# Latent attention interleaved with the mLSTM heads, and mLSTM products padded to 128 rows

## The chip, the cores and the metric

The kernel runs on one core of a Trainium2 chip. The metric is the time of one execution on the device, in microseconds (us). The core has a matrix engine (TensorE, PE in the profile; PEld is its weight load), a vector engine (VectorE, DVE), a scalar engine (ScalarE, ACT), a general engine (GpSimd, POOL) and SyncE (SP), which issues most of the transfers here. Each engine runs its own instructions in order and waits for the others through semaphores.

## What is computed

Two blocks of two layers each, on 512 tokens of 1024 features. The change lies in the first block's mixer, which runs once in each of its two layers. The mixer projects its input into three branches, concatenates their outputs and multiplies by `w_out`; a mixture of 16 experts follows. Cut to the two branches that matter here:

```python
def _mla(...):                       # latent attention, 8 heads, 64 + 32 features for q and k
    q = rmsnorm(c_q) @ w_uq;  kv = rmsnorm(c_kv) @ w_ukv
    s = q_nope @ k_nope + q_rope @ k_rope      # k_rope is shared by all heads
    y_a = softmax(s * scale) @ v

def _mlstm_scan(q, k, v, ig, lf):    # 4 heads of 64 features, run forward and backward
    qk  = (q @ k.T) * w_intra        # inside a chunk
    num = qk @ v + w_inter * (q @ C) # C: state carried from chunk to chunk
    h   = num / max(abs(den), exp(-m))
```

The third branch (a state-space scan, `ssd_` in the code) ends before the stage of interest.

## The kernel before

The 512 tokens are four tiles of 128 (`NT = 4`), and products of the projections are made of three fp16 products each (`mm3`, lines 147 to 151), since every fp32 operand is split into a high and a low fp16 half (`split`, lines 143 and 144; `wsplit` for weights, lines 133 and 134). A layer's `mixer1` runs: projection of latents and gates, the `ssd_` branch, `mlstm_proj` (its last product is `gvo`), then four times `mlstm_head`, then `mla`, then `proj_out` (`gO`). The code is written in this order, but a scheduler fixes the order of instructions on each engine when the program is built, so neighbouring parts overlap. Tiles come from pools with a fixed number of buffers: a tile's next use waits until all readers of the old one are done. PSUM tiles have tags: `acc` and `acm` (sums of projections, `sM`), `s` (`diag`, `sT`) and `o` (`lo`, `o`, `mxT`, `mixT`), two buffers each.

`mlstm_head` (one head h): heads 0 and 1 lie in partitions 0 to 63 and 64 to 127 of the same tiles, as do 2 and 3; `r` is the head's half. `vw` (L1016) and `mlU` (L1022) give the chunk states, which ACT (L1030) and DVE (L1032) chain into `mst`, in the half `r` only. `decays` loads `dk` by a transfer on SP (L856), POOL adds two masks (L859), ACT takes exponentials (L862). `blocks` makes `diag` (L870), four products of 64 rows, which DVE multiplies into `dk` (L1039). For each direction, `lo` sums `dk` times `v` (L1044, 128 rows) and, for three of four tiles, `qs` times `mst` (L1046, 64 rows). DVE then makes the denominator (L1050 to L1053) and writes `mo` (L1056, or L1059 and L1060). An fp32 product stands as two instructions in the trace. `mlstm_norm` normalises a pair of heads, `mix_part` transposes it (`mixT`) into `mT`, the operand of `gO`.

`mla` splits its weights, makes values (`gV`), and goes through four groups of two heads. `project(g)` makes `gQ`, `gK` and the maxima over keys (`sM`, `mx` on DVE, `mxT`). Then, for each head, `softmax_T` makes scores `sT`, `pe` and `pt` (L748, L751, L752), and `pv` makes `o`. The shared rope part of the keys is copied into `Kt` (`mlak`) by eight POOL copies (L672). Group g + 1 is projected ahead of the softmax of group g. The argument `also` of `mla` runs the normalisation of the second mLSTM pair after the first projection.

Of the kernel before, what the change touches and what calls it, by code (L numbers as in the profile page):

```python
# [11 lines left out]
F32 = mybir.dt.float32  # L12
F16 = mybir.dt.float16
BF16 = mybir.dt.bfloat16
I32 = mybir.dt.int32
AF = mybir.ActivationFunctionType
# [5 lines left out]
P = 128  # L22
T = 512
NT = 4
# [21 lines left out]
class Kern:  # L46
# [374 lines left out]
    def mixer1(self, l, cur):  # L421
        p1 = self.p1
        pr = self.params1(l)
        xh, xl = cur["xT"]
        self.mT = self.xT_tiles(p1, "mT")
        u = 1.0 / (AS * WS_IN)

        def load(key, i, n):
            return [self.wload(self.ap[key][l, i, h] if i is not None else self.ap[key][l, h],
                               4 * n, WS_IN) + (4,) for h in range(2)]  # L430

        r = lambda name: self.pool(name, side="right")
        cA = load("wA", None, 472)
        with self.pool("la") as la:
            with r("qa") as self.qa:
                with r("gp") as self.gp:
                    pa = self.qa.tile([P, NT, 472], F32, name="pa")
                    ss = p1.tile([P, 2, NT], F32, name="ss")
                    junk = self.gp.tile([P, 256], F32, tag="g4", name="junk")
                    for t in range(NT):  # L440
                        ps = self.tm_gemm(xh, xl, cA, 472, t, "gA", "acc")
                        self.nc.scalar.activation(pa[:, t, :], ps[:, :472], AF.Copy, scale=u)
                        self.nc.scalar.activation(junk[:, :256], pa[:, t, 0:256], AF.Square,
                                                  accum_out=ss[:, 0, t:t + 1])
                        self.nc.scalar.activation(junk[:, :128], pa[:, t, 256:384], AF.Square,
                                                  accum_out=ss[:, 1, t:t + 1])
                    with ExitStack() as es:
                        for i in cur.get("after", ()):
                            es.enter_context(self.tc.issue_after(i))
                        cD = load("wB", 2, 512)  # L450
                        cC = load("wB", 1, 512)
                    self.gates1(l, pr, pa)
                lat = self.mla_latents(la, pr, pa, ss)
            with r("qm") as qm, r("m1") as m1:
                with r("s1") as self.q1, r("s2") as s2:
                    sd = self.ssd_tiles()
                    for b in (2, 4, 0, 3, 5, 1):
                        self.ssd_conv(b, pr, xh, xl, cC, cD, sd, u)
                    self.ssd_gate(xh, xl, cC, sd, u)
                    c0, c1 = (self.ssd_core(s2, m1, g, pr, sd, u) for g in range(2))  # L460
                    for c in (c0, c1, c0, c1, c0, c1, c0, c1):
                        next(c, None)
                cE = load("wB", 3, 512)
                cB = load("wB", 0, 512)
                ml = self.mlstm_proj(qm, pr, xh, xl, cE, cB, u)
                mo = [self.p2.tile([P, NT, P], F32, tag="mo", name="mo", bufs=2) for i in range(2)]
                og = ml[-1]
                for h in range(4):
                    self.mlstm_head(m1, h, mo[h // 2], *ml)
                    if h > 1:  # L470
                        (self.mlstm_norm(0, mo[0], og) if h == 2 else self.mix_part(p1, 4, mo[0]))
                with r("ml") as p:
                    self.ptp, self.npt = p, (6, 2)
                    self.mla(p, l, lat, lambda: (self.mlstm_norm(1, mo[1], og), self.mix_part(p1, 5, mo[1])))

    def gates1(self, l, pr, pa):

# [173 lines left out]
                self.split(krh[0][64:128], krh[1][64:128], ps[64:128], AS)  # L651
        return cq, ckv, krh

    def mla(self, p1, l, lat, also):
        nc, p2 = self.nc, self.p2
        cq, ckv, krh = lat
        wq = [self.wload(self.ap["w_uq"][l], 2048, WS_UQ) + (2,)]
        wkv = [self.wload(self.ap["w_ukv"][l], 1024, WS_UKV) + (1,)]
        v = self.values(p1, "mlav", 8, 64, 0, 8)
        for t in range(NT):  # L660
            ps = self.acc("gV")
# [3 lines left out]
        scale = 96.0 ** -0.5  # L665
        HG = 2
        Q, K = {}, {}

        Kt = [[p1.tile([P, T], F16, name="mlak%d%d" % (h, i)) for i in range(2)] for h in range(4)]
        for h in range(4):  # L670
            for i in range(2):
                nc.gpsimd.tensor_copy(Kt[h][i][64:128], krh[i][64:128])  # L672

        def project(g):

# [19 lines left out]
            return mrow  # L695

        mrow = project(0)
        also()
        for g in range(8 // HG):
            nrow = project(g + 1) if (g + 1) * HG < 8 else None  # L700
            for i, h in enumerate(range(g * HG, (g + 1) * HG)):
                pt = self.softmax_T(
                    lambda s, ps, st: [
                        self.mm3(ps, K[h][0][:, s * P:(s + 1) * P], K[h][1][:, s * P:(s + 1) * P],
                                 Q[h][0], Q[h][1], True, False),
                        nc.tensor.matmul(ps, self.sel[:, i, :], mrow, start=False, stop=True)],
                    scale, [0] * NT, v[0] is None)
                o = self.pso("o")
                for t in range(NT):
                    self.pv(o[:, t * 66:t * 66 + 65], [(pt[s], t, self.value(v, s, h)) for s in range(NT)])  # L710
                if h % 2 == 0:
                    mx_ = p2.tile([P, NT, P], F32, tag="mo", name="mo", bufs=2)
                self.norm_out(o, 66, 64, mx_[:, :, 64 * (h % 2):64 * (h % 2) + 64])
                if h % 2:
                    self.mix_part(p1, h // 2, mx_)
            mrow = nrow
# [282 lines left out]
    def mlstm_head(self, p1, h, mo, q, k, kt, v, og):  # L999
        nc, p2 = self.nc, self.p2  # L1000
        i, r = h // 2, slice(64 * (h % 2), 64 * (h % 2) + 64)
        if h % 2 == 0:

            self.qs = p1.tile([P, 2, T], F32, tag="mqs", name="mqs", bufs=2)
            for j in range(2):
                nc.sync.dma_start(self.qs[64 * j:64 * j + 64].rearrange("p d t -> p (d t)"),
                                  self.d_wi[h + j:h + j + 1].rearrange("h d t -> h (d t)").partition_broadcast(64))
            for d_ in range(2):
                ts = slice(P * (1 - d_), P * (4 - d_))
                nc.vector.tensor_tensor(self.qs[:, d_, ts], self.qs[:, d_, ts], q[i][:, ts], op=ALU.mult)  # L1010
            self.mst = p1.tile([P, NT, 2, 66], F32, tag="mst", name="mst", bufs=2)

        vw = p1.tile([P, NT, 2, 66], F32, tag="vw", name="vw", bufs=1)
        for d_ in range(2):
# [3 lines left out]
        ps, c, U = self.psx("mlU"), 0, {}  # L1018
# [8 lines left out]
        for d_ in range(2):  # L1027
            ts = (1, 2, 3) if d_ == 0 else (2, 1, 0)
            step = 1 if d_ == 0 else -1
            nc.scalar.activation(self.mst[r, ts[0], d_], U[ts[0] - step, d_], AF.Copy)  # L1030
            for t in ts[1:]:
                nc.vector.scalar_tensor_tensor(self.mst[r, t, d_], self.mst[r, t - step, d_],  # L1032
                                               self.dec[r, 2 * d_, h, t - step:t - step + 1], U[t - step, d_],
                                               op0=ALU.mult, op1=ALU.add)
        dk = self.decays(p1, self.d_nc[0], h, 0)
        ps = self.blocks(k[i][r], q[i][r])
        for d_ in range(2):
            e = dk[:, d_].rearrange("p c i -> p (c i)")
            nc.vector.tensor_tensor(e, ps, e, op=ALU.mult)  # L1039
            o = self.pso("lo")  # L1040
            for t in range(NT):
                inter = self.DST[t][0] <= d_ < self.DST[t][1]
                c = slice(t * 66, t * 66 + 65)
                nc.tensor.matmul(o[:, c], dk[:, d_, t], v[:, t, h, :65], start=True, stop=not inter)  # L1044
                if inter:
                    nc.tensor.matmul(o[:, c], self.qs[r, d_, t * P:(t + 1) * P], self.mst[r, t, d_, :65],  # L1046
                                     start=False, stop=True)
            o3 = o[:, :NT * 66].rearrange("p (t d) -> p t d", t=NT)
            den = self.sm.tile([P, NT, 1], F32, tag="den", name="den")
# [943 lines left out]
```

## Time and profile before

| | us |
|---|---|
| median of 3 runs (lowest to highest) | 2487.95 (2486.26 to 2492.34) |
| the profiled execution, its span | 2485.69, 2483.9 |
| PE busy | 2268.1 (91%) |
| DVE busy | 1698.7 (68%) |
| ACT busy | 1163.8 (47%) |
| POOL busy | 241.0 (10%) |

The span is one execution's from first to last instruction; the shares are means over stages with different limits. Matmuls are pipelined and their ends are modelled, so the distance between two starts says more of PE than a duration does. The stage of the change, from the last `gvo` to the end of the latent attention, lies at 162.6 to 290 us in layer 0 and at 704.1 to 835.5 us in layer 1.

### The profile page before, as it was taken

The numbers are of one execution on the slowest core, as the hardware profiler recorded it, in microseconds if no ns is written. First come the engines' busy times: TensorE is split into PE (matmuls) and PEld (weight loads), VectorE is DVE, ScalarE is ACT, GpSimd is POOL, SyncE is SP. The second block draws the span as 40 slices with busy tenths as digits, with TensorE's granted clock in tenths as the row PEclk, the third lists the DMA queues.
The fourth block names the chain that finished last, engine by engine and source line by source line (L and its number), as shares of the span: only waits on it lengthen the run. The fifth ranks groups of instructions, "written<-read, shape, count | busy, mean of one in ns | idle before, by whom it ended". The sixth has DMA issues, their size and how long they took to land.

```text
span 2483.9 us, 34670 instructions
## 1 busy us (share of the span) xinstructions
PE 2268.1 (91%) x13330; PEld 1239.8 (50%) x13334; DVE 1698.7 (68%) x3668; ACT 1163.8 (47%) x1981; POOL 241.0 (10%) x295
## 2 busy tenths in 40 slices
PE   7898979888898979879898899999998989999999
PEld 4554545544564545534455654444444556544444
DVE  7968887778949877768999664442469996644421
ACT  5534737755625637834554543331245546333321
POOL 1220022221200013221000100000000000000000
PEclk9988989999979979989999999999999999999999
DMA  5320458973210549953210152222331101522222
GB/s 181 122 74 1 166 188 261 338 246 103 96 66 18 213 152 313 341 182 105 80 53 35 49 209 106 102 102 77 119 132 52 52 34 60 187 102 102 102 77 77
DMA packets 57695, 315.25 MB, mean 127 GB/s; under 512 B 9652, under 2 KB 9908, under 8 KB 29104
## 3 DMA queue, kind: packets, MB, share of 16 engines
q1 hardware_dynamic: 40448, 263.67, 29.7%
q0 software_dynamic: 12464, 32.48, 5.2%
q10 hardware_dynamic: 4608, 16.78, 1.8%
q8 instruction: 108, 1.77, 0.3%
q14 instruction: 67, 0.55, 0.1%
HBM read 286.59 MB, written 30.90 MB: 128 GB/s over the span
## 4 chain that ended last, share of the span: by engine, by line
PE 39%; DVE 10%; ACT 4%; issue 2%; DMA 1%; DVEq 0%; ACTq 0%
PE fd L149 3%; PE fd L151 3%; PE fd L150 3%; PE fu L151 3%; PE fg L151 3%; PE fg L150 3%; PE fu L150 3%; PE fg L149 3%; PE fu L149 3%; PE o L787 2%; DVE wl L134 1%; PE gqk L149 1%; DVE mx L1784 1%; PE gqk L151 1%; PE gqk L150 1%
## 5 line engine op out<-in xcount | busy, mean ns | idle before, releaser
L134 DVE SCALAR_TENSOR_TENSOR wl<-wst,wh 128x1024 f16<-128x1024 f32 (+1 forms) x428 | 517.2, 1236 | 211.4 <-ACT wh L133 210.1
L133 ACT ACTIVATE wh<-wst 128x1024 f16<-128x1024 f32 (+1 forms) x428 | 430.0, 1048 | 283.4 <-PE fd L151 107.0
L150 PEld LDWEIGHTS <-wh 128*128 128x128 f16 x968 | 96.1, 99 | 105.4 <-issue 8.3
L151 PEld LDWEIGHTS <-wl 128*128 128x128 f16 x968 | 96.0, 99 | 102.9 <-issue 4.7
L149 PEld LDWEIGHTS <-wh 128*128 128x128 f16 x968 | 96.0, 99 | 101.7 <-issue 4.6
L149 PE MATMUL fd<-wh,fhh 128*128 128x512 f16 x352 | 133.4, 379 | 0.0
L150 PE MATMUL fd<-wl,fhh 128*128 128x512 f16 x352 | 133.4, 379 | 0.0
L151 PE MATMUL fd<-wh,fhl 128*128 128x512 f16 x352 | 133.4, 379 | 0.0
L149 PE MATMUL gqk<-wh,xTh 128*128 128x512 f16 x320 | 123.0, 384 | 6.5 <-ACT rsq L1668 6.2
L150 PE MATMUL gqk<-wl,xTh 128*128 128x512 f16 x320 | 123.0, 384 | 0.0
L151 PE MATMUL gqk<-wh,xTl 128*128 128x512 f16 x320 | 122.8, 384 | 0.0
L149 PE MATMUL fg<-xTh,wh 128*128 128x512 f16 x320 | 121.3, 379 | 0.0
L150 PE MATMUL fg<-xTl,wh 128*128 128x512 f16 x320 | 121.3, 379 | 0.0
L151 PE MATMUL fg<-xTh,wl 128*128 128x512 f16 x320 | 121.3, 379 | 0.0
L149 PE MATMUL fu<-xTh,wh 128*128 128x512 f16 x320 | 121.3, 379 | 0.0
L150 PE MATMUL fu<-xTl,wh 128*128 128x512 f16 x320 | 121.3, 379 | 0.0
L151 PE MATMUL fu<-xTh,wl 128*128 128x512 f16 x320 | 121.3, 379 | 0.0
L150 PEld LDWEIGHTS <-xTh 128*128 128x128 f16 x768 | 74.8, 99 | 70.4 <-issue 12.2
L149 PEld LDWEIGHTS <-xTh 128*128 128x128 f16 x768 | 74.7, 99 | 68.2 <-ACT xTh L143 5.8
L151 PEld LDWEIGHTS <-xTl 128*128 128x128 f16 x768 | 74.4, 99 | 64.6 <-issue 3.5
L149 PE MATMUL gO<-wh,mTh 128*128 128x512 f16 x256 | 98.4, 385 | 2.8 <-ACT mTh L143 2.8
L1843 DVE SCALAR_TENSOR_TENSOR fth<-fth,fg 128x512 f32<-128x512 f32 x40 | 27.5, 687 | 107.5 <-ACT fth L1842 107.5
(612 smaller groups left out, 5516.9 us busy)
## 6 DMA issues: line engine op xcount, KB each, us to landing
wst<-in_w_gu SPq DMA_DIRECT2D x108, 1024.0 KB, 6.2
wst<-in_w_dn SPq DMA_DIRECT2D x52, 1024.0 KB, 9.7
wst<-in_w SPq DMA_DIRECT2D x28, 1024.0 KB, 4.8
wst<-in_wB SPq DMA_DIRECT2D x16, 1024.0 KB, 4.9
wst<-in_w_out SPq DMA_DIRECT2D x16, 1024.0 KB, 4.8
dk<-d_nc SPq DMA_DIRECT2D x16, 512.0 KB, 3.7
rows<-xrow SPq DMA_DIRECT2D x8, 512.0 KB, 2.6
res<-xa SPq DMA_DIRECT2D x8, 512.0 KB, 2.7
```

What stands on the lines that cost most here:

```text
L133: nc.scalar.activation(wh[:, a:b], st[:, a:b], AF.Copy, scale=scale)
L134: (eng or nc.vector).scalar_tensor_tensor(wl[:, a:b], st[:, a:b], scale, wh[:, a:b], op0=ALU.mult, op1=ALU.subtract)
L149: mm(out, ah, bh, start=start, stop=False)
L150: mm(out, ah, bl, start=False, stop=False)
L151: mm(out, al, bh, start=False, stop=stop)
L787: mm(out, p[:, bs], v, start=first, stop=last)
L1784: nc.vector.tensor_reduce(mr[:, t, h:h + 1], ps[:, :n], axis=AX.X, op=ALU.max)
L1843: nc.vector.scalar_tensor_tensor(th, th, 1.0, pg, op0=ALU.add, op1=ALU.mult)
```

## The change

`mla` becomes a generator that stops ahead of each of its four groups. `mixer1` starts it first (weights, values, the first projection), and then takes mLSTM heads and attention groups in turn. The eight key copies move to the front of `mla`. In `mlstm_head`, the operands `q` and `mst` get a zeroed other half, made by POOL, so that `diag` and the second product of `lo` run over 128 rows; `mst` becomes one tile per head. `pt` has five buffers instead of six, and the attention's `mo` moves to a pool with one buffer of its own. The `ml` pool, which holds `Kt`, `pt` and the new `mqz` (one buffer), opens ahead of the heads.

```diff
@@ mixer1
-                for h in range(4):
-                    self.mlstm_head(m1, h, mo[h // 2], *ml)
-                    if h > 1:
-                        (self.mlstm_norm(0, mo[0], og) if h == 2 else self.mix_part(p1, 4, mo[0]))
                 with r("ml") as p:
-                    self.ptp, self.npt = p, (6, 2)
-                    self.mla(p, l, lat, lambda: (self.mlstm_norm(1, mo[1], og), self.mix_part(p1, 5, mo[1])))
+                    self.ptp, self.npt = p, (5, 2)
+                    mla = self.mla(p, l, lat)
+                    next(mla)
+                    for h in range(4):
+                        self.mlstm_head(m1, h, mo[h // 2], *ml)
+                        if h > 1:
+                            (self.mlstm_norm(0, mo[0], og) if h == 2 else self.mix_part(p1, 4, mo[0]))
+                        if h == 3:
+                            self.mlstm_norm(1, mo[1], og)
+                        next(mla, None)
+                    self.mix_part(p1, 5, mo[1])
+                    for _ in mla:
+                        pass
@@ mla
+        Kt = [[p1.tile([P, T], F16, name="mlak%d%d" % (h, i)) for i in range(2)] for h in range(4)]
+        for h in range(4):
+            for i in range(2):
+                nc.gpsimd.tensor_copy(Kt[h][i][64:128], krh[i][64:128])
...
         mrow = project(0)
-        also()
         for g in range(8 // HG):
+            yield
             nrow = project(g + 1) if (g + 1) * HG < 8 else None
...
-                    mx_ = p2.tile([P, NT, P], F32, tag="mo", name="mo", bufs=2)
+                    mx_ = p1.tile([P, NT, P], F32, tag="mo", name="mo")
@@ mlstm_head
-            self.mst = p1.tile([P, NT, 2, 66], F32, tag="mst", name="mst", bufs=2)
+        z = slice(64 * (1 - h % 2), 64 * (1 - h % 2) + 64)
+        qz = self.ptp.tile([P, T], F32, tag="mqz", name="mqz")
+        nc.gpsimd.memset(qz[z], 0.0)
+        nc.gpsimd.tensor_copy(qz[r], q[i][r])
+        mst = p1.tile([P, NT, 2, 66], F32, tag="mst", name="mst", bufs=2)
+        nc.gpsimd.memset(mst[z], 0.0)
...
-        ps = self.blocks(k[i][r], q[i][r])
+        ps = self.blocks(k[i], qz)
...
-                    nc.tensor.matmul(o[:, c], self.qs[r, d_, t * P:(t + 1) * P], self.mst[r, t, d_, :65],
+                    nc.tensor.matmul(o[:, c], self.qs[:, d_, t * P:(t + 1) * P], mst[:, t, d_, :65],
                                      start=False, stop=True)
```

What the scheduler makes of it shows in the order of instructions. On PE, right behind `gvo`, the heads stood together before (`mv` is v, `mqs` is `qs`):

```order
L1044 MATMUL lo<-mv,dk 128x65 x2
L870 MATMUL diag<-ml_1312,ml_1366 128x128 x2
L1046 MATMUL lo<-mst,mqs 128x65
L1044 MATMUL lo<-mv,dk 128x65 x2
L1022 MATMUL mlU<-vw,mkt 128x66
L870 MATMUL diag<-ml_1339,ml_1399 128x128
L1046 MATMUL lo<-mst,mqs 128x65
L1044 MATMUL lo<-mv,dk 128x65
```

In the changed kernel, all of `gV` and the first projection come first, and the first head's `lo` (now L1058 and L1060) stands between the second projection and the first scores:

```order
L736 MATMUL mxT<-idf,mx 128x128 x4
L1058 MATMUL lo<-mv,dk 128x65 x2
L1060 MATMUL lo<-mst,mqs 128x65
L1058 MATMUL lo<-mv,dk 128x65
L1060 MATMUL lo<-mst,mqs 128x65
L1058 MATMUL lo<-mv,dk 128x65
L1060 MATMUL lo<-mst,mqs 128x65
L151 LDWEIGHTS wl
L151 MATMUL gQ<-cq_586,wl 128x512
L1058 MATMUL lo<-mv,dk 128x65
L714 LDWEIGHTS sel
L714 MATMUL sT<-mrow,sel 128x512
```

Each head's products thus moved from one block behind `gvo` into a gap of the attention's. On DVE, the first head's denominator stood among other instructions of the heads:

```order
L1050 TENSOR_SCALAR den<-lo 128x4
L1032 SCALAR_TENSOR_TENSOR mst<-mst,dec,mlU 64x66
L1051 TENSOR_TENSOR den<-den,lo 128x4
L1032 SCALAR_TENSOR_TENSOR mst<-mst,dec,mlU 64x66
L1052 TENSOR_TENSOR den<-den,flo 128x4
L1039 TENSOR_TENSOR dk<-diag,dk 128x512
L1053 RECIPROCAL den<-den 128x4
L1050 TENSOR_SCALAR den<-lo 128x4
L1056 TENSOR_TENSOR mo<-lo,den 128x4x64
```

Now (L1064 to L1070) it stands among the attention's products and a weight split:

```order
L1064 TENSOR_SCALAR den<-lo 128x4
L1046 SCALAR_TENSOR_TENSOR mst<-mst,dec,mlU 64x66
L1065 TENSOR_TENSOR den<-den,lo 128x4
L690 TENSOR_TENSOR qtmp<-gQ,tab 128x512
L1066 TENSOR_TENSOR den<-den,flo 128x4
L134 SCALAR_TENSOR_TENSOR wl<-wst,wh 128x1024
L1067 RECIPROCAL den<-den 128x4
L1064 TENSOR_SCALAR den<-lo 128x4
L1070 TENSOR_TENSOR mo<-lo,den 128x4x64
```

The attention's `qtmp` moved up between the chain's steps. On POOL, the additions of the last two heads (`dk`) and the memsets of `mx` followed the key copies directly:

```order
L672 COPY mlak_1883<-krh_591 64x512
L859 TENSOR_TENSOR dk<-dk,m_lt 128x512
L859 TENSOR_TENSOR dk<-dk,m_gt 128x512
L859 TENSOR_TENSOR dk<-dk,m_lt 128x512
L859 TENSOR_TENSOR dk<-dk,m_gt 128x512
L720 MEMSET mx 128x512 x3
```

Now the padding stands among them, in the same queue:

```order
L1022 MEMSET mqz 64x512
L1023 COPY mqz<-ml_1312 64x512
L728 MEMSET mx 128x512
L1025 MEMSET mst 64x528
L867 TENSOR_TENSOR dk<-dk,m_lt 128x512
L867 TENSOR_TENSOR dk<-dk,m_gt 128x512
L728 MEMSET mx 128x512
L1022 MEMSET mqz 64x512
L1023 COPY mqz<-ml_1339 64x512
L1025 MEMSET mst 64x528
```

The third head's additions now stand behind the second head's `mqz` and the memset of `mst`, and the memsets of `mx` alternate with them.

## Rows read from the trace of the kernel before

**Rows 1.** Windows, layer 0: stretch, length, busy PE PEld DVE ACT POOL, clock, DMA.
```profile
162.60:205.00 42.40, 41.08 (x194) 32.35 (x193) 24.10 (x82) 12.54 (x47) 5.28 (x4) 0.71 0.14 50
205.00:213.00 8.00, 5.70 (x19) 2.21 (x18) 7.03 (x21) 3.01 (x5) 0.00 (x0) 0.71 0.00 0
213.00:290.00 77.00, 69.26 (x653) 36.09 (x651) 69.31 (x130) 52.87 (x105) 2.71 (x5) 0.99 0.16 56
162.60:290.00 127.40, 116.03 (x862) 70.66 (x860) 100.43 (x233) 68.42 (x157) 7.99 (x9) 0.88 0.15 50
```

**Rows 2.** The same windows of layer 1.
```profile
704.10:750.00 45.90, 44.58 (x191) 34.89 (x189) 22.59 (x81) 12.54 (x47) 5.15 (x4) 0.63 0.12 46
...
757.00:835.50 78.50, 70.27 (x656) 36.69 (x655) 70.22 (x132) 53.29 (x106) 2.69 (x5) 0.98 0.16 55
704.10:835.50 131.40, 119.55 (x859) 73.41 (x858) 98.37 (x231) 68.24 (x157) 7.83 (x9) 0.84 0.14 49
```

**Rows 3.** Windows in the heads of layer 0; the clock is the number before DMA's.
```profile
170.00:175.00 5.00, 5.00 (x34) 3.98 (x32) 3.47 (x14) 0.22 (x1) 0.00 (x0) 1.00 0.25 93
180.00:185.00 5.00, 5.00 (x20) 4.00 (x20) 1.77 (x8) 1.52 (x6) 0.00 (x0) 0.50 0.27 97
```

**Rows 4.** Timeline of PE, heads of layer 0: start us, us, instruction, count.
```profile
170.67 0.44 PE L1044 MATMUL lo<-mv,dk 128*128 128x65 f32 x2
171.04 0.43 PE L1046 MATMUL lo<-mst,mqs 64*128 64x65 f32 x2
...
180.21 0.69 PE L1044 MATMUL lo<-mv,dk 128*128 128x65 f32 x2
180.83 0.69 PE L1046 MATMUL lo<-mst,mqs 64*128 64x65 f32 x2
```

**Rows 5.** Timeline of PE: fp32 products of 128 rows and of 64.
```profile
118.75 1.00 PE L932 MATMUL so<-xs,spe 128*128 128x64 f32 x8
119.58 0.38 PE L151 MATMUL gE<-xTh,wl 128*128 128x512 f16 x1
...
99.60 1.28 PE L870 MATMUL diag<-bc 128*128 128x128 f32 x10
...
163.06 1.16 PE L870 MATMUL diag<-ml,ml 64*128 64x128 f32 x10
```

**Rows 6.** Lines 720 and 672: duration in ns, min/median/max.
```profile
L720 POOL MEMSET mx<- x16: 524/524/543, 5.3 to 2057.7; 128x512 f32 x16
...
L672 POOL COPY mlak<-krh x16: 604/623/1624, 132.8 to 677.6; 64x512 f16<-64x512 f16 x16
```

**Rows 7.** Timeline of POOL in the heads of layer 0.
```profile
176.13 1.27 POOL L859 TENSOR_TENSOR dk<-dk,m_lt 128x512 f32<-128x512 f32 x1 [37.58 <-DMA dk<-d_nc]
...
186.12 1.27 POOL L859 TENSOR_TENSOR dk<-dk,m_lt 128x512 f32<-128x512 f32 x1 [7.37 <-ACT mst L1030]
```

**Rows 8.** Timeline of DVE in the heads of layer 0.
```profile
173.59 0.36 DVE L1016 TENSOR_TENSOR vw<-mv,wec 128x198 f32<-128x198 f32 x1
...
175.17 0.42 DVE L1060 TENSOR_TENSOR mo<-mo,ltmp 128x256 f32<-128x256 f32 x1
...
176.38 1.24 DVE L1016 TENSOR_TENSOR vw<-mv,wec 128x198 f32<-128x198 f32 x1
...
186.22 1.45 DVE L1060 TENSOR_TENSOR mo<-mo,ltmp 128x256 f32<-128x256 f32 x1
```

**Rows 9.** Timeline of ACT in the attention.
```profile
228.60 0.63 ACT L751 ACTIVATE pt<-pe 128x512 f16<-128x512 f32 x1
```

**Rows 10.** Waits of SP's queue, 260 to 560 us: us in total, times, longest.
```profile
SPq L122 <- DVE eth L1418: 21.1, 2, 18.5
```

**Rows 11.** Timeline of DVE, first head of layer 0.
```profile
169.16 0.16 DVE L1050 TENSOR_SCALAR den<-lo 128x4 f32<-128x4 f32 x1 [1.48 <-PE lo L1046]
...
172.68 0.41 DVE L1056 TENSOR_TENSOR mo<-lo,den 128x256 f32<-128x256 f32 x1
```

More of the change, by code (lines that the diff above doesn't have):

```diff
@@ L652, in mla_latents, with mla @@
         return cq, ckv, krh
-    def mla(self, p1, l, lat, also):
+    def mla(self, p1, l, lat):
         nc, p2 = self.nc, self.p2
         cq, ckv, krh = lat
+        Kt = [[p1.tile([P, T], F16, name="mlak%d%d" % (h, i)) for i in range(2)] for h in range(4)]
+        for h in range(4):
+            for i in range(2):
+                nc.gpsimd.tensor_copy(Kt[h][i][64:128], krh[i][64:128])
         wq = [self.wload(self.ap["w_uq"][l], 2048, WS_UQ) + (2,)]
@@ L667, in mla @@
         Q, K = {}, {}
[L669 to L672, printed above, removed]
         def project(g):
@@ L1029, in mlstm_head @@
             step = 1 if d_ == 0 else -1
-            nc.scalar.activation(self.mst[r, ts[0], d_], U[ts[0] - step, d_], AF.Copy)
+            nc.scalar.activation(mst[r, ts[0], d_], U[ts[0] - step, d_], AF.Copy)
             for t in ts[1:]:
-                nc.vector.scalar_tensor_tensor(self.mst[r, t, d_], self.mst[r, t - step, d_],
+                nc.vector.scalar_tensor_tensor(mst[r, t, d_], mst[r, t - step, d_],
                                                self.dec[r, 2 * d_, h, t - step:t - step + 1], U[t - step, d_],
```

## The prediction

> **What bounds the kernel now.** I read the windows of each layer's mixer first, from the last `gvo` product to the end of the latent attention: 162.6 to 290 us in layer 0 and 704.1 to 835.5 us in layer 1 [rows 1, 2]. The reader should see two halves. In the first, the four mLSTM heads, PE is busy nearly all the time (41.08 of 42.40 us, 44.58 of 45.90) while DVE works only 24.10 and 22.59 us. In the last, the attention's groups, DVE and PE are each busy 90% (69.31 and 69.26 of 77.00 us), and DVE, whose busy time is not stretched by modelled ends, sets the pace. Over the whole stage DVE works 100.43 of 127.40 us and 98.37 of 131.40 us: 27.0 + 33.0 = 60.0 us in which the second half's bound stands idle, most of it in the first half.
>
> Then the PE timeline of the heads, for why PE is full there. PE's clock is not the same throughout: 1.00 in 170 to 175 us, then 0.50, the lower of the two levels, in 180 to 185 us [rows 3]; ahead of the fall PE had been busy all the time, but with small fp32 products that alternate between 128 rows (L1044) and 64 rows (L1046). A pair of instructions of either kind starts 0.37 us after the pair before it at full clock, and 0.62 us at half clock [rows 4]. Eight instructions of nearly the same size that are all 128 rows (`so`, 64 columns) take 119.58 - 118.75 = 0.83 us, so 0.21 us a pair [rows 5]. Alternating costs 0.16 us a pair at full clock and, against 0.42, 0.20 us at half clock.
>
> The Trainium skill, page "TensorEngine Tiling (Array Packing)", section "Tiling Modes", says that changing the tiling mode drains TensorE. The trace agrees [rows 4, 5]: by the rule the padded products go at 0.21 us a pair, which is what the rows gave without it.
>
> **The change part by part.**
>
> *Padding.* Per layer, 4 heads x 2 directions x (4 + 3) products x 2 instructions = 112 instructions, 56 pairs, of which about 48 stand at a switch: 48 x 0.16 = 7.7 us of PE at full clock. Ten `diag` products of 64 rows took 1.16 us and ten of 128 rows 1.28 us [rows 5], 0.012 us each, so the 32 padded ones per layer cost at most 0.4 us: nothing. PE's work in the heads, told in full-clock time, is 41.08 x 0.71 = 29.2 us [rows 1]; less 7.7 it is 21.5, below DVE's 24.10. For the whole stage: 116.03 x 0.88 - 7.7 = 94.4 us and 119.55 x 0.84 - 7.7 = 92.7 us, both below DVE's 100.43 and 98.37 [rows 1, 2]. So DVE becomes the bound of the stage, if the order lets it.
>
> *Interleaving.* It adds no DVE, ACT or PE work. It puts the attention's DVE work (products' maxima, splits) into the heads' stretch, and the heads' short chains between them; the order of DVE and PE shows it. What share can DVE then reach? The nearest row is the stretch where this already happens with other work, 0.90 (69.31 of 77.00; 70.22 of 78.50 in layer 1). At 0.90 the stages last 111.6 and 109.3 us: -15.8 and -22.1, together -37.9 us. PE then needs 94.4 of 111.6 us, 0.85, less than the 0.90 it shows now in that stretch. The bounds are a share of 1.00 (-60.0 us) and today's 0.79 and 0.75 (nothing).
>
> *POOL.* New per layer: four `mqz` memsets and four copies, and four `mst` memsets, two of which stand ahead of the stage. A 128x512 fp32 memset took 0.524 us and a 64x512 fp16 copy 0.623 [rows 6]; the fp32 copy I bound above by POOL's 128x512 fp32 addition, 1.27 us [rows 7]. Six memsets and four copies: 5.6 to 8.2 us of POOL. POOL itself is idle there, so the cover is its own idle time. But DVE pays: while POOL ran its additions at 176.13 and 186.12 us, a `vw` product of 0.36 us took 1.24 and a `mo` addition of 0.42 took 1.45 [rows 7, 8]: 1.9 us lost to 5.28 us of POOL work. At that rate 2.0 to 3.0 us per layer; I take 3. The eight `mlak` copies stand at the same place in POOL's queue as before, ahead of the stage; that edit is worth nothing.
>
> *Buffers.* Five `pt` tiles instead of six, and one `mo` tile for the attention instead of two: no row shows the wait. Below: nothing. Above: each of 8 heads waits once for a conversion of 0.63 us [rows 9], 5 us per layer. PE and DVE now have the heads' work to fill such a gap, so I take 1 us.
>
> *What comes behind.* The stage's end frees the memory for the experts' weights, which therefore move with it. They are early: with its buffers full, SP waits up to 18.5 us until the first expert's DVE work frees one [rows 10]. So a shorter stage starts the experts earlier and nothing there takes the gain back. In SP's queue the fourth head's `dk` load now stands behind the last `w_out` load; that needs only a split which DVE does early, so the cost is nothing; without that cover the last head would wait for one split more.
>
> Sum: -37.9 + 2 x 3 + 2 x 1 = -29.9 us. The profiled execution took 2485.7 us (span 2483.9), 2.3 below the median, so about 2455.8 for it and **2458 us** against the median of 2488. A measurement here tells about 0.3%, 7.5 us, from no change.
>
> **The rivals.**
>
> *POOL takes its whole time from DVE* (0.20). The skill's page "SBUF — State Buffer", section "SBUF: two separate sides", says that VectorE and GpSimd share a port pair under an exclusive lock, held for the whole instruction; by that rule every added POOL instruction could stop DVE for its length, and the two stretched DVE rows agree. Worked out from rows: 8.2 us per layer instead of 3, and with it the buffers at their 5 us: -37.9 + 16.4 + 10 = -11.5, 2476 us. Against it: two of the four POOL additions stretched nothing, and many of DVE's instructions here read PSUM.
>
> *The clock stays as low as now* (0.10). If PE goes on at a mean of 0.88 and 0.84 [rows 1, 2], because it waits for DVE from the start as in 205 to 213 us (0.71, 5.70 of 8.00 us busy), its work takes 94.4 / 0.88 = 107.3 and 92.7 / 0.84 = 110.4 us, at its 0.90 share 119.2 and 122.7: -16.9 + 8 = -9, 2479 us. Against it: 0.99 and 0.98 in the attention's stretch with PE busy 90%.
>
> *Slower: the two `o` buffers in PSUM* (0.10). The heads' `lo` sums and the attention's `o`, `mxT` and `mixT` share two buffers. A `lo` buffer is held from its sum until L1056 has read it: DVE's first reader ran at 169.16 and L1056 ended at 173.09 us [rows 11], 3.9 us. DVE's new order puts more between these two. If each of 8 `lo` sums per layer stopped PE, and so DVE, for these 3.9 us, that is 31.4 us per layer: -29.9 + 62.8 = +33, 2521 us. It decides from 15 / 8 = 1.9 us a sum. Against it: the other buffer stays free meanwhile, and there is other work in front of the next use.
>
> **How the numbers follow.** Forecast 0.60, rivals 0.20, 0.10, 0.10. The forecast's own range is 2444 to 2472. The range asked for reaches down to a DVE share of 0.95 (-49.6 us, 2438) and up to where the first two rivals end, 2484; outside lie the slower case and the tails. Faster: 0.60 + 0.15 of the first rival + 0.05 of the second = 0.80. Within 0.3%: the rest of these two, 0.10. Slower: 0.10.
>
> **What would show it.** In the profile after: windows from the last `gvo` to the end of the attention of 110 to 115 us in place of 127.4 and 131.4, with DVE at 0.88 or more; the lower clock nearly gone from them; `lo` pairs 0.21 us apart; DVE instructions stretched beside `mqz` copies, 2 to 3 us per layer; the experts' stretch as long as before. I am wrong if DVE's share stays near 0.8: then the waits named for DVE tell which rival it is (`lo` or `o` for the buffers, a low clock with PE full for the second, long DVE instructions with no wait for the first).

## The result, and the profile after

The changed kernel took 2458.14 us (median of 5 runs, 2453.0 to 2459.86), the kernel before 2486.92 us on the same chips: a ratio of 0.988 (0.986 to 0.990). The forecast was 2458 us. The profiled execution has a span of 2451.2 us, 32.7 less than before. The stage's windows, with the columns of [rows 1]; the end is again the start of the last `mixT` (836.2 us in layer 1 of before):

```profile
163.80:205.00 41.20, 32.73 (x216) 18.50 (x214) 36.19 (x74) 21.64 (x45) 5.65 (x7) 0.92 0.19 64
...
240.00:276.90 36.90, 35.37 (x381) 23.21 (x380) 32.68 (x85) 20.60 (x49) 1.14 (x2) 1.00 0.26 87
163.80:276.90 113.10, 100.66 (x892) 62.79 (x890) 100.54 (x232) 68.19 (x156) 13.26 (x17) 0.97 0.17 57
...
691.80:805.90 114.10, 102.17 (x891) 64.14 (x889) 100.19 (x231) 68.40 (x156) 13.23 (x17) 0.96 0.16 56
...
276.90:567.60 290.70, 245.50 (x1489) 142.46 (x1490) 222.30 (x482) 176.27 (x248) 69.28 (x62) 0.92 0.74 246
805.90:1085.50 279.60, 229.83 (x1371) 135.09 (x1371) 209.74 (x450) 165.35 (x224) 64.39 (x52) 0.88 0.76 256
```

The windows of the kernel before that answer to the last three:

```profile
704.10:836.20 132.10, 120.25 (x861) 73.62 (x860) 98.89 (x232) 68.24 (x157) 7.83 (x9) 0.84 0.14 49
...
290.00:580.00 290.00, 250.09 (x1522) 146.22 (x1521) 223.81 (x482) 175.53 (x247) 61.76 (x62) 0.92 0.74 247
836.20:1116.60 280.40, 228.20 (x1400) 134.12 (x1399) 209.15 (x449) 164.08 (x223) 66.54 (x52) 0.90 0.76 255
```

The reader is to see three things. DVE does the same work (100.54 against 100.43 us in layer 0), but its share rose from 0.79 to 0.89, and in the first part, where it had worked 24.10 of 42.40 us [rows 1], it works 36.19 of 41.20. The stage is 14.3 us shorter in layer 0 and 18.0 in layer 1, together 32.3 of the 32.7. And what follows it, to the same place in the program, takes as long as before (290.7 for 290.0, 279.6 for 280.4). The lengths of the stages repeat well: from the start of the last `gvo` to that of the last `mixT`, both layers together, they come to 227 to 229 us in the three traces with this order (this one, changed_again and pool_copies below). What lies between the two stages doesn't: it took some 414 us here and 421 in changed_again, the same kernel. So experiments on the stage are read from its windows first.

Who waits for `lo` shows where most of DVE's idle time went. This is the view of that tile on PE, in the kernel before (us, times):

```profile
L1046 PE MATMUL lo<-mst,mqs x96: 219/414/475, 166.0 to 749.6; 64*128 64x65 f32 x96
...
  DVE den L1050: 34.7, 16
```

and in the changed kernel:

```profile
L1060 PE MATMUL lo<-mst,mqs x96: 220/275/276, 181.1 to 793.3; 128*128 128x65 f32 x96
...
  DVE den L1064: 3.9, 6
```

DVE's waits for `lo` fell from 34.7 to 3.9 us over both layers. PE's timeline in the fourth head, with starts of pairs 0.22 us apart where they were 0.37 or 0.62 [rows 4]:

```profile
261.18 0.39 PE L1060 MATMUL lo<-mst,mqs 128*128 128x65 f32 x2
261.41 0.39 PE L1058 MATMUL lo<-mv,dk 128*128 128x65 f32 x2
261.63 0.39 PE L1060 MATMUL lo<-mst,mqs 128*128 128x65 f32 x2
```

A new wait stands in the stage too, at 184 to 194 us; the timeline over all engines:

```profile
184.48 0.33 SPq L864 DMA_DIRECT2D dk<-d_nc  x1
...
188.97 1.27 POOL L867 TENSOR_TENSOR dk<-dk,m_lt 128x512 f32<-128x512 f32 x1 [4.10 <-DMA dk<-d_nc]
...
189.56 2.90 DVE L760 TENSOR_TENSOR pt<-pe,pt 128x512 f16<-128x512 f32 x2
190.19 1.71 POOL L867 TENSOR_TENSOR dk<-dk,m_gt 128x512 f32<-128x512 f32 x1
190.27 1.28 ACT L870 ACTIVATE dk<-dk,ubc 128x128 f32<-128x128 f32 x4 [4.64 <-POOL dk L867]
...
193.12 0.61 ACT L143 ACTIVATE mlaq<-qtmp 128x512 f16<-128x512 f32 x1
...
193.79 0.61 PE L698 MATMUL sM<-mlak,mlaq 128*128 128x512 f16 x1 [5.43 <-ACT mlaq L143]
```

The third head's `dk` can be loaded only when the first head's `lo` (184.06 us) has freed one of two buffers. ACT has that head's exponentials next in its queue and waits 4.64 us; the split of `mlaq` behind them is ready, but comes at 193.12, and PE waits 5.43 us for it. In layer 1 it is the same.

### The profile page after: what moved, and what is told of

It is laid out like the page before. It is cut to its first block, busy times and chain, and to the rows that moved or that the text cites. A ratio compares the mean times of both kernels' runs of the same rounds, so it can differ in the third digit from the quotient of the medians.

```text
span 2451.2 us, 34696 instructions
## 1 busy us (share of the span) xinstructions
PE 2233.7 (91%) x13334; PEld 1220.2 (50%) x13334; DVE 1699.8 (69%) x3668; ACT 1165.9 (48%) x1981; POOL 263.0 (11%) x319
## 4 chain that ended last, share of the span: by engine, by line
PE 39%; DVE 10%; ACT 4%; issue 2%; DMA 2%; DVEq 0%; ACTq 0%
PE fd L151 3%; PE fd L149 3%; PE fd L150 3%; PE fg L150 3%; PE fu L150 3%; PE fu L149 3%; PE fg L149 3%; PE fu L151 3%; PE fg L151 3%; PE o L795 2%; DVE wl L134 1%; PE gqk L149 1%; DVE mx L1798 1%; PE gqk L151 1%; PE gqk L150 1%
## 5 line engine op out<-in xcount | busy, mean ns | idle before, releaser
L134 DVE SCALAR_TENSOR_TENSOR wl<-wst,wh 128x1024 f16<-128x1024 f32 (+1 forms) x428 | 511.9, 1223 | 206.2 <-ACT wh L133 205.5
```

What stands on the lines that cost most here:

```text
L134: (eng or nc.vector).scalar_tensor_tensor(wl[:, a:b], st[:, a:b], scale, wh[:, a:b], op0=ALU.mult, op1=ALU.subtract)
```

## The experiments

Times are medians in us; each ratio is to the kernel before on the same chip. The first four runs shared a chip, so did the next four, and the last three.

| run | time | ratio (95% interval) |
|---|---|---|
| pad_alone | 2464.73 | 0.992 (0.989 to 0.995) |
| inter_alone | 2471.37 | 0.993 (0.991 to 0.996) |
| late_exp | 2448.40 | 0.985 (0.982 to 0.988) |
| pool_copies | 2458.53 | 0.989 (0.986 to 0.993) |
| lo_pad | 2450.09 | 0.987 (0.985 to 0.990) |
| lo_pad_pt6 | 2447.34 | 0.987 (0.984 to 0.989) |
| pool_adds | 2463.01 | 0.993 (0.991 to 0.995) |
| pt4 | 2455.55 | 0.989 (0.987 to 0.991) |
| changed_again | 2459.52 | 0.988 (0.986 to 0.990) |
| gate_copies | 2449.35 | 0.984 (0.982 to 0.986) |
| gate_both | 2449.54 | 0.983 (0.981 to 0.985) |

**pad_alone** is the kernel before with the padding:

```diff
-        ps = self.blocks(k[i][r], q[i][r])
+        ps = self.blocks(k[i], qz)
...
-                    nc.tensor.matmul(o[:, c], self.qs[r, d_, t * P:(t + 1) * P], self.mst[r, t, d_, :65],
+                    nc.tensor.matmul(o[:, c], self.qs[:, d_, t * P:(t + 1) * P], mst[:, t, d_, :65],
```

> The kernel before with the padding alone: the heads stand in one block as before, diag and the second product of lo run over 128 rows (mqz, one mst tile per head), the attention is unchanged with six pt buffers. If the stage was bound as I said (PE in the heads, by 7.7 us of switches at full clock and about 10 us at half), the heads shorten by 8 to 12 us per layer and the rest of DVE's idle time there stays: about 2467 us (2462 to 2472). Rival A, the whole gain is the padding, because the low clock came from the alternating products: heads of 27 us (24.1 at a DVE share of 0.9), 15 us per layer, 2457 us. Rival B, the heads are a chain of short DVE steps and PE's time is no bound: 2483 to 2488 us.

Its windows: the end of the heads in layer 0, and the two stages.

```profile
190.00:205.00 15.00, 10.29 (x38) 6.01 (x37) 10.76 (x34) 3.41 (x7) 0.00 (x0) 0.67 0.00 0
...
161.60:279.20 117.60, 103.51 (x866) 63.50 (x865) 101.30 (x233) 68.77 (x157) 12.41 (x17) 0.94 0.16 54
699.80:816.80 117.00, 103.58 (x866) 63.00 (x864) 99.75 (x233) 68.83 (x157) 12.61 (x17) 0.94 0.16 55
```

The time is inside my range. The stages are 9.8 and 15.1 us shorter than before, 24.9 of the 32.3 us. (The run has one `mst` tile per head too; inter_alone keeps that and turns back the padding alone.) The clock still falls to 0.67 in the heads, now with PE busy 10.29 of 15 us: a low clock comes without a single alternating product too. Rival A's price of 15 us came true in layer 1 and not in layer 0. By times alone the changed kernel can't be told from this run: the intervals of pad_alone and of pool_copies, the changed kernel's equal, overlap. The stages tell them apart, 117.6 and 117.0 us for 113.1 and 114.1.

**inter_alone** is the changed kernel with these two lines turned back, and without `mqz` and the memsets.

> The changed kernel without the padding: diag and the second product of lo run over 64 rows again, without mqz and without the memsets; the order of instructions stays that of the changed kernel. My sum: PE then needs 102.1 and 100.4 us at full clock in stages of 111.6 us, a share of 0.91, about what it reached before, so DVE still sets the pace and most of the gain stays: 2458 to 2466 us. Rival A (padding is the gain): 2473 us or more, with the clock low again where lo alternates. Rival C (POOL's padding work takes DVE's time): faster than the changed kernel, by 6 to 16 us, 2442 to 2452 us.

Windows of the two stages, and two of the fourth head, layer 0 and layer 1:

```profile
162.30:281.50 119.20, 106.99 (x892) 65.95 (x889) 101.22 (x232) 68.19 (x156) 8.32 (x9) 0.99 0.15 54
...
699.60:824.20 124.60, 112.60 (x891) 68.70 (x890) 101.64 (x232) 68.27 (x156) 8.29 (x9) 0.93 0.15 52
...
265.00:270.00 5.00, 5.00 (x29) 3.65 (x29) 2.40 (x10) 1.53 (x3) 0.00 (x0) 1.00 0.38 161
805.00:810.00 5.00, 5.00 (x17) 3.79 (x16) 1.21 (x3) 1.17 (x2) 0.00 (x0) 0.50 0.06 21
```

and who waited for `lo`:

```profile
L1055 PE MATMUL lo<-mst,mqs x96: 272/321/473, 179.6 to 809.2; 64*128 64x65 f32 x96
...
  DVE den L1059: 17.7, 16
```

The time is above my range. The stages are 8.2 and 7.5 us shorter than before, with DVE at 0.85 and 0.82. PE's mean share is 0.90, as I had reckoned. The mean clock is 0.99 and 0.93, so not low throughout as in rival A; yet in layer 1 it fell to 0.50 while the fourth head's sums alternated, and the same sums of layer 0 ran at 1.00. DVE waits for all 16 `lo` sums, 17.7 us in place of 3.9. A sum is a chain of seven pairs, and 0.15 us more for each pair makes 1.05 us a sum, an estimate of 16.8 us for 16. A mean share of PE doesn't show that. In full-clock time PE's work is 106.99 x 0.99 - 100.66 x 0.97 = 8.3 us above the changed kernel's in layer 0 and 6.6 in layer 1: the padding's term of 7.7 holds (the rounded clock alone leaves either about 1 us open).

**late_exp** holds back ACT's exponentials of the third and fourth head:

```diff
-            nc.scalar.activation(mrow, self.max_rows(mx), AF.Copy)
+            self.mrs.append(nc.scalar.activation(mrow, self.max_rows(mx), AF.Copy))
...
-        dk = self.decays(p1, self.d_nc[0], h, 0)
+        with self.tc.issue_after(self.mrs[h - 1].ins) if h > 1 else nullcontext():
+            dk = self.decays(p1, self.d_nc[0], h, 0)
```

> The changed kernel with one order fixed: ACT's exponentials of the third and fourth head's dk come behind the mrow copy of the group before, not ahead of the splits of mlaq. In the trace of the changed kernel ACT stood 4.64 us ahead of the third head's exponentials (190.27 us), because dk could be loaded only when the first head's lo had freed its buffer (issue 184.48, landing 188.97), and a split of mlaq behind it kept PE idle for 5.4 us and DVE for 3 to 4 us. If DVE is the bound of the stage and this wait is a true loss, both layers give 3 to 5 us: about 2450 us. Rival: DVE makes the time up from other ready work, or the exponentials are now late for the heads: 2456 to 2462 us.

```profile
161.20:270.10 108.90, 100.18 (x890) 62.31 (x889) 99.87 (x232) 67.76 (x156) 13.27 (x17) 0.98 0.17 59
...
689.80:799.00 109.20, 100.20 (x890) 62.42 (x889) 100.02 (x232) 67.75 (x156) 13.24 (x17) 0.98 0.17 59
```

Both stages are 4 to 5 us shorter than the changed kernel's, and 3 to 4 than those of pool_copies. All 6 runs (2444.35 to 2453.9) lie below the middle of pool_copies' on the same chip. The two stages together, counted as above, are 218 to 220 us long in each of the five traces with this order (late_exp, lo_pad, lo_pad_pt6, gate_copies, gate_both), against 227 to 229. The wait was a true loss.

**pool_copies** puts a loop of three rounds around `mqz`'s memset and copy.

> The changed kernel with mqz's memset and copy made three times over by POOL, 2 x (0.52 + 0.61) = 2.3 us more for each head, 9 us per layer. If these two kinds of POOL instruction leave DVE alone (no DVE instruction beside them was longer than its like in the changed kernel's trace), the time stays: 2455 to 2462 us. Rival C, POOL takes its whole time from DVE: 18 us more, 2476 us; at the rate of the additions (1.9 us lost for 5.28): 6.5 us more, 2465 us.

```profile
163.00:275.65 112.65, 100.68 (x892) 62.73 (x889) 100.15 (x232) 68.18 (x156) 20.14 (x29) 0.97 0.16 57
689.80:802.02 112.22, 99.98 (x892) 62.51 (x889) 100.43 (x232) 68.18 (x156) 20.12 (x29) 0.98 0.16 57
```

POOL works 20.14 us instead of 13.26 and DVE's busy time stays (100.15): where this work stands, it takes next to nothing from DVE. That is a matter of what stands beside it. In pt4 (below) a copy of `mqz` meets a `pt` subtraction, which else takes 0.68 us, and in the changed kernel a memset ahead of layer 1's stage meets a step of 0.16 us:

```profile
204.99 0.60 POOL L1023 COPY mqz<-ml 64x512 f32<-64x512 f32 x1
205.02 1.12 DVE L760 TENSOR_TENSOR pt<-pe,pt 128x512 f16<-128x512 f32 x1
...
666.28 0.52 POOL L1022 MEMSET mqz<- 64x512 f32 x1
666.34 0.49 DVE L972 TENSOR_SCALAR ssda<-ssda 128x4 f32<-128x4 f32 x1
```

**lo_pad** is late_exp without `mqz`, with `diag` at 64 rows; **lo_pad_pt6** gives the room to a sixth `pt` buffer; **pt4** is the changed kernel with four:

```diff
-                    self.ptp, self.npt = p, (5, 2)
+                    self.ptp, self.npt = p, (6, 2)
```

> late_exp with the padding of lo's second product alone: diag runs over 64 rows again, mqz with its memsets and copies is gone; the orders of DVE and ACT stay the same row for row. My theory: the padding pays where products of the two kinds alternate, in lo (48 of the switches per layer); diag's four products stand together, so leaving them at 64 rows adds two switches per block, 8 x 0.16 = 1.3 us of PE per layer beside DVE's work: the time of late_exp, 2446 to 2452 us. Rival: the diag products count as well (DVE waits for them before it makes dk): 2453 us or more. If POOL's mqz work cost DVE something, the time falls below 2444 us.

> lo_pad with six pt buffers instead of five, in the memory that mqz left. The prediction put five buffers and one mo tile at 1 us per layer, with a bound of 5 us. By the waits in late_exp's trace (no wait of PE, ACT or DVE for a pt buffer is longer than 1.1 us) the sixth buffer brings 0 to 1 us per layer: 2445 to 2450 us. Rival, the upper bound: 2438 to 2443 us.

> The changed kernel with four pt buffers instead of five, which is one head's four tiles with none to spare. The prediction put the loss of one pt buffer and one mo tile together at 1 us per layer: then 2460 us, 2457 to 2463. Rival, the upper bound of one conversion of 0.63 us per head: 2468 us. With four, a head's scores can't start before the head ahead has used its first tile, so above 2475 us would say that the fifth buffer carries the interleaving.

All three came out within 3 us of what the kernel they derive from took (pt4 1.5 us below its range), and no step between four, five and six buffers can be told from nothing. So padding `diag` and the fifth buffer are not what the time hangs on. lo_pad and pt4 are set against kernels of other chips, with ratios of 0.987 for 0.985 and 0.989 for 0.988 and intervals that overlap; lo_pad's two stages are 218.7 us long, late_exp's 219.7. The `mo` pool with one buffer was not tried by itself.

**pool_adds** repeats POOL's two mask additions for the mLSTM's `dk`, on top of late_exp.

> late_exp with POOL's mask additions of the mLSTM's dk made twice (the mask is -1e30, so the exponentials are the same): 8 x 1.27 = 10.2 us more of POOL per layer. In the trace of the changed kernel a DVE instruction with two SBUF operands was stretched beside such an addition (two pt subtractions took 2.90 us instead of 1.29 at 189.56 us), while nothing was stretched beside memsets and copies. If DVE pays for additions at the rate so far (1.9 us for 5.28): 3.7 us per layer, 2455 us (2452 to 2459). Rival, POOL takes its whole time: 10 us per layer, 2468 us. Rival, nothing, because most of DVE's instructions here read PSUM: 2448 us.

It missed: 2463, above the 2455 that I named and below the 2468 of the first rival. The two stages, and groups of DVE's instructions in the first of them (busy us, mean ns):

```profile
167.40:280.90 113.50, 100.56 (x892) 62.32 (x891) 103.41 (x232) 67.87 (x156) 19.50 (x21) 0.98 0.17 57
701.70:813.80 112.10, 100.59 (x893) 62.32 (x892) 102.98 (x232) 67.65 (x156) 19.47 (x21) 0.98 0.17 57
...
L761 DVE TENSOR_TENSOR pt<-pe,pt 128x512 f16<-128x512 f32 x32 | 24.2, 770 | 1.0 <-ACT pt L760 0.9
...
L144 DVE SCALAR_TENSOR_TENSOR mlaq<-qtmp,mlaq 128x512 f16<-128x512 f32 x8 | 6.5, 818 | 0.3 <-ACT mlaq L143 0.3
...
L701 DVE TENSOR_SCALAR mx<-mx 128x8 f32<-128x8 f32 x4 | 1.7, 425 | 0.0
```

In late_exp these three have means of 735, 684 and 159 ns. DVE's busy time in the stages is 3.5 and 3.0 us above late_exp's, for the 5.1 us of additions that two heads add: 0.6 to 0.7 of them, where I had assumed 1.9 for 5.28, or 0.36. And the additions of the other two heads run at 121 to 134 us, ahead of the stage, where ACT's queue waits for them (14.4 us in 100 to 168 us, 8.7 in late_exp) and the last `gvo` starts some 6 us later (167.4 for 161.1). I had counted all four heads inside the stage. The remark in the expectation that nothing was stretched beside memsets and copies holds inside the stage alone.

**gate_copies** and **gate_both** are lo_pad with POOL's work taken out of that earlier stretch:

```diff
+                    self.gate = self.nc.gpsimd.tensor_copy(tick, ml[2][:, 1, 0, 0:1]).ins
...
-                nc.gpsimd.tensor_copy(Kt[h][i][64:128], krh[i][64:128])
+                with self.tc.issue_after(self.gate):
+                    nc.gpsimd.tensor_copy(Kt[h][i][64:128], krh[i][64:128])
...
-        with self.tc.issue_after(self.mrs[h - 1].ins) if h > 1 else nullcontext():
+        with self.tc.issue_after(self.mrs[h - 1].ins if h > 1 else self.gate):
```

> The changed kernel as it is, on the chip of the two runs after it, so that they can be set against it directly: 0.988 of the kernel before (0.986 to 0.990). If lo_pad's and late_exp's 0.985 to 0.987 were only the chip, the runs after it stand no lower than this one.

> lo_pad with the eight mlak copies of POOL held back behind the last mkT copy (a one-element POOL copy reads mkt first). In late_exp's trace these copies ran from 131.11 to 137.03 us, and small DVE steps of 0.16 us beside them (ssd_rsq, 128 x 4) took 0.52 us, although POOL's mqz copies had stretched nothing in the stage of the change. If a copy stops DVE whenever DVE's operands are all in SBUF, some nine such steps lose 0.36 us each, 3.2 us per layer in a stretch where DVE is busy 99%: 6 us less than lo_pad, 2444 us, about 0.985. Behind 140 us DVE is busy a third of the time. Rival: those steps wait for each other, not for POOL, and nothing changes: the time of lo_pad.

> gate_copies with POOL's mask additions of the first two heads held back behind the same one-element copy. In late_exp's trace they ran from 120.75 to 126.65 us, and three DVE instructions of 0.55 us beside them (mqs, xs) took 1.62 us each, 3.2 us in all, while ACT waited 4.6 us for the first of them. If DVE's stretch there is the path to the end, as 19.83 of 20 us busy says: 3 us per layer and 6 us less than gate_copies, 2438 us, about 0.982 to 0.983. Rival: the additions come too late for the first head (its dk is wanted at 169.9 us), or stretch the stage's splits instead: no better than gate_copies, or worse.

Timeline of DVE and POOL in late_exp:

```profile
121.98 1.58 POOL L868 TENSOR_TENSOR dk<-dk,m_gt 128x512 f32<-128x512 f32 x1
...
122.36 1.62 DVE L965 TENSOR_TENSOR xs<-xs,sti 128x384 f32<-128x384 f32 x1
...
131.11 5.92 POOL L669 COPY mlak<-krh 64x512 f16<-64x512 f16 x8 [4.47 <-DVE ssd_rsq L166]
...
132.18 0.52 DVE L168 SCALAR_TENSOR_TENSOR ssd_rs<-ssd_rsq,ssd_rs 128x4 f32<-128x4 f32 x1
```

and in gate_both:

```profile
123.85 0.55 DVE L968 TENSOR_TENSOR xs<-xs,sti 128x384 f32<-128x384 f32 x1
...
130.64 0.16 DVE L168 SCALAR_TENSOR_TENSOR ssd_rs<-ssd_rsq,ssd_rs 128x4 f32<-128x4 f32 x1
...
137.85 1.26 POOL L871 TENSOR_TENSOR dk<-dk,m_gt 128x512 f32<-128x512 f32 x1
...
137.94 1.19 DVE L167 TENSOR_TENSOR ssd_rsq<-ssd_rsq,ssda 128x4 f32<-128x4 f32 x1
```

With POOL's work gone the same instructions take 0.55 and 0.16 us, and where it went, a step of 0.16 us takes 1.19. The mechanism is shown; a gain from it is not. DVE's steps of the same chain (`ssd_rsq` to `xs`) now run beside the moved work in part, and PE still waits for their result:

```profile
142.45 0.33 PE L293 MATMUL mixT<-idf,xs 128*128 128x128 f32 x1 [2.27 <-DVE xs L979]
```

That is gate_copies. In lo_pad PE waited 3.20 us at an earlier product of this chain (136.95 us), and in gate_both 4.33 (143.01 us). The last `gvo` of layer 0 starts at 159.8 us in gate_copies and at 162.1 in gate_both, against 160.3 in lo_pad; two traces of the changed kernel have 163.8 and 161.4, so 2 us is no difference here. Both times are above the 2444 and 2438 that I expected, on a chip whose kernel before is 5.7 us slower than lo_pad's; the ratios of 0.984 and 0.983 are about those expected, but stand beside late_exp's with intervals that overlap. On its own chip gate_copies is 10.2 us below the changed kernel, as late_exp is 10.1 below pool_copies on another. Whether the gates bring anything stays open.

## Why the prediction was right, point by point

**The bound.** Right. DVE sets the pace of the stage: its work is nearly the same and the stage shrank until its share was 0.89 and 0.88. I had a share of 0.90 and then 4 us per layer for POOL and the buffers, so stages of 115.6 and 113.3 us; 113.1 and 114.1 came. In late_exp, without the one large wait that I had not seen, they are 108.9 and 109.2, where 0.90 alone says 111.6 and 109.3.

**Padding and interleaving.** The sum was right, but the gain was put down wholly to the interleaving, with the padding as what makes PE's work fit. Alone, the padding shortens the stages by 24.9 us, more than three quarters of the whole, and the interleaving by 15.7; together 32.3. They are two ways to the same idle time of DVE, and each leaves what the other takes: without the padding DVE waits for long `lo` sums, without the interleaving it has too little to do between them. The step that failed is "PE then needs 94.4 of 111.6 us", read without its counterpart: 102 us would have fitted as well, and did not suffice, since the mean share says nothing of a wait for one chain. The 7.7 us of the padding measured 8.3 and 6.6 us of PE's work. The Trainium skill, page "TensorEngine Tiling (Array Packing)", section "Tiling Modes", holds that a change of mode drains TensorE; the trace agrees (0.37 us a pair alternating, 0.22 not; the drain itself has no row).

**POOL.** The term of 3 us per layer was too large. POOL worked 5.3 us more in layer 0's stage (13.26 for 7.99). DVE's busy time grew by 0.1 us there and by 1.3 in layer 1, and three times the work changed nothing. What failed is the rate, 1.9 us lost for 5.28, carried over from additions to memsets and copies: for the additions it was even 0.6 to 0.7 (pool_adds), and beside the new work nothing was lost. DVE's instructions there mostly read PSUM (`dk` from `diag`, `mlavl` from `gV`); where one with both inputs in SBUF had begun first, the copy took longer instead (1.09 us for 0.61, at 206.60 us). My rival took the rule too widely. The Trainium skill, page "SBUF — State Buffer", section "SBUF: two separate sides", limits the lock to a DVE instruction in a two-port mode, or one with two SBUF inputs against a GpSimd instruction that reads SBUF. The trace agrees: of the rows above, `pt`, `mlaq`, `xs` and `ssd_rs` read SBUF twice and were stretched beside additions or copies. `mx` (0.16 to 1.23 us beside an addition) and `ssda` (0.16 to 0.49 beside a memset) read it once; in which mode they ran, no run here shows. No reader of PSUM was stretched in any trace. The stage's only such loss in the changed kernel is beside the additions, 2.2 and 1.9 us in the two layers, where it was 1.9 and 0.6 before; layer 1's 1.3 us are this.

**Buffers.** The term of 1 us named the wrong tile. `pt` costs nothing that can be measured, but `dk` with its two buffers does: the interleaving moved the first head's `lo` to 181 us and with it the third head's load, and ACT's order put the exponentials in front of work that was ready. That costs 3 to 5 us per layer, which late_exp gives back. So two terms were wrong by about the same amount with opposite signs (4 us for POOL and `pt`, about 1 found; none for `dk`, 3 to 5 found), and that the sum came so close is in this part luck.

**What comes behind.** Right in sum: the experts' stretch moved with the stage's end and grew by nothing, 290.7 for 290.0 us, as far as one trace of each tells.

**The rivals.** Low clock: 0.97 and 0.96, with one fall to 0.66 in layer 0 at 190 to 200 us, where PE waited for `mlaq`. The `o` buffers: PE waits for none in the tile view of `lo`. POOL: above.

**The better version.** late_exp takes 2448 us, 10 less than pool_copies, the changed kernel's equal, on the same chip. gate_copies, which contains its edit among others, has all runs (2444.3 to 2449.4) below all of changed_again's (2453.65 to 2461.55).

## What to carry to other kernels

Where two parts of a kernel are bound by different engines, look for the engine that idles in one and is full in the other: its total work, over the share that it reaches where it is full, forecast the stages after interleaving to within 5 us here. Then look for chains that it waits for one by one, since a mean share of PE below 1 does not say that they are short enough. And after a reordering check each load whose buffer is freed by work that has moved: its first reader may stand in an in-order queue ahead of work that is ready.

## What the runs showed of the hardware

A pair of fp32 products that alternates between 64 and 128 rows starts 0.37 us after the last, one that does not 0.22, both at the clock of 1.00; ten products of 64 rows in a row take 1.16 us and ten of 128 rows 1.28 [rows 5]. DVE and POOL hold each other up when both work in SBUF as above: a 128 x 4 step of 0.16 us became 0.52 beside a copy of 64x512 fp16 and 1.19 beside an addition of 128x512 fp32. What made the clock of 0.50 in the heads of before stays open: alternating products among other work left it at 1.00 in layer 0 of inter_alone and had 0.50 in layer 1, and the padded heads, with PE waiting, had 0.67.
